# A hybrid transformer block on one core: inputs in the host's layouts, and a start without transposes of x

## The chip, the cores and the metric

The kernel runs on one core of one Trainium2 chip. The metric is the device time of one execution in microseconds (us), the median of several runs. A profile was taken of one further execution; its trace has the start and length of each instruction on the engines TensorE (PE), VectorE (DVE), ScalarE (ACT) and GpSimd (POOL), of SyncE (SP) and of the DMA queues.

## What is computed

One layer of a block over 256 tokens of 2048 features, in float32. Cut to what matters:

```
h = rms_norm(x, mix_norm)
proj = h @ w_in                               # 2048 -> 10320 columns
dn_q, dn_k, dn_v, dn_z, dn_b, dn_a, mla_q, mla_ckv, mla_kr, gate_a, gate_b = split(proj)
# branch A: conv of 4 taps + SiLU on q, k, v; l2-normed q, k; gated delta rule in chunks of 64
q_a, k_a = l2norm(cq), l2norm(ck)
o_a = gated_delta_rule(q_a, k_a, v_a, g, beta)      # holds a triangular solve in each chunk
# branch B: attention over a compressed KV latent, block-causal mask
o_b = mla_attention(qn, qr, kn, kr, v_b)
y = sigmoid(gate_a) * (o_a @ w_branch_a) + sigmoid(gate_b) * (o_b @ w_branch_b)
x = x + y @ w_out
x = x + square(relu(rms_norm(x, mlp_norm) @ w_mlp_up)) @ w_mlp_down     # 2048 -> 8192 -> 2048
x = x + sigmoid(rms_norm(x, ple_norm) @ w_ple_gate) * (p @ w_ple)
```

where `rms_norm(x, g)` is `x * rsqrt(mean(x * x) + eps) * g`.

## The kernel before

**The stream.** All weights pass through one loop, `stream(groups)`. A *group* is one product of 256 tokens with 512 columns of a weight (464 in the first group, 384 in the query groups of branch B), and a *step* is two blocks of 128 rows of its weight: a raw tile of 128 x 2 x 512 floats, 512 KB, that SP loads (`load`, five raw buffers). `cut` splits it three steps ahead: ACT casts it to the fast float format (`whi`, a group at L102, the line through which all ACT and DVE instructions are recorded), and DVE subtracts (`wlo`). The activations are held in the same way, high and low. A product takes three matmuls, high by high, high by low and low by high, so a step has 12 matmuls of up to 512 columns (L392; L385 and L388 for groups with the operands turned). There are 540 steps. Sums of a group lie in two banks of a PSUM pool of four; the other pool of four serves everything else (`bank`).

**Side work.** Between steps `weave` lets one of four lanes of generators go on: L_TURN (making the activations), L_CONV (convolutions of q, k, v and loading of parameters), L_SOLVE (the triangular solve and the delta rule) and L_MLA. A scheduler then sets each engine's order, by the program's order and by what waits for what. Up to the point where the row statistic `rx` is known, ACT and DVE keep strictly to the program's order (`act.on`, `dve.on`).

**The start.** x is loaded with tokens on the partitions in four pieces (`load_x`) between the first raw tiles. TensorE turns it, 32 transposes of 128x128 (`tp_hT`, L269). ACT scales the result by the gain `mix_norm` into the high part of `hT` and DVE makes the low part. The gains come as rows of a small tile (`gmix`) and are turned too (`tp_mix`). The sum of squares of each token comes from ACT's squares of x with a running sum (`junk_x`), and `rx` is its rsqrt by Newton steps on DVE. `rx` is applied where a group leaves PSUM. The first group's `evac_first` begins with `until(lambda: "rx" in done)`, so the program's order puts all that leads to `rx` ahead of the second group. The first group carries the columns of the decay gates; their sums over tokens, `gsum` (L713), go to TensorE as 12 small matmuls. The first group's sums are used by branch A and B; after the second group, the third is of 384 columns.

**The middle.** Each of k, q, v is convolved in two halves (`conv`). For k, TensorE turns the result to tokens (`tp_tmk`, L757), ACT squares it (`junk_k`), DVE takes the rsqrt (`l2k`, `l2kv`, `l2ky`, `rk`) and multiplies (`tmk`), and TensorE turns it back (`tp_kT`, L781), the operand of `kk` (L820). The triangular solve sends diagonal blocks through DRAM by GpSimd's queue and back (`there`, to `blk`), works them row by row on DVE (`blk`), and sends the results back (`back`, to `ro`), from which DVE masks the diagonal blocks (`d`).

**Parameters.** Gains, conv weights, a_log, dt_bias, rope gains and positions come as twelve small loads in `load_rest`, behind the rest of the constants; the gains and conv weights are turned on TensorE (`gain_columns`).

The two lines that set the order around the change are these:

```
            until(lambda: "rx" in done)           # first line of evac_first
            if k0 + 2 >= g.nk: g.evac(ps)         # in stream: a group leaves at its last step
```

Of the kernel before, what the change touches and what calls it, by code (L numbers as in the profile page):

```python
# [9 lines left out]
F32 = mybir.dt.float32  # L10
# [30 lines left out]
NPIECE = 5  # L41

# [47 lines left out]


# [17 lines left out]
def hybrid_block(ctx: ExitStack, tc: tile.TileContext, a, dbg=None):  # L109
# [3 lines left out]
    x, out = a["x"][0], a["out"][0]  # L113
    w_in = a["w_in"][0]
# [32 lines left out]

    cst = cpool.tile([P, CST.shape[1]], F32, name="cst")
    nc.sync.dma_start(cst[:, :P], a["cst"][:, :P])
    gmix = big("gmix", shape=(KD, P))  # L150
    nc.scalar.dma_start(gmix, a["mix_norm"][0].rearrange("(r p) -> r p", p=P))
# [9 lines left out]

    rows = (("mlp_norm", 16), ("ple_norm", 16), ("ckv_norm", 4),
            ("dn_out_norm", 1), ("q_nope_norm", 1), ("k_nope_norm", 1))
    nrows = sum(n for _, n in rows)
    rowt = big("rowt", shape=(P, 2, P))
    grow, crow = rowt[:nrows, 0, :], rowt[:96, 1, :]
    gcol, r0 = {}, 0
    for name, n in rows:
        gcol[name] = r0
        r0 += n  # L170
    gains = cpool.tile([P, nrows + KD], F32, name="gains")
    gcol["mix_norm"] = nrows
    convw = cpool.tile([P, 96], F32, name="convw")
    hw = cpool.tile([P, 16], F32, name="hw")
    rg = cpool.tile([P, 2, ROPE], F32, name="rg")
    posi = cpool.tile([P, NT], I32, name="posi")

    def load_rest():
        def load(dst, src):
            tc.keep_in_program_order(nc.sync.dma_start(dst, src))  # L180

        load(cst[:, P:], a["cst"][:, P:])
        yield
        for name, n in rows:
            r0 = gcol[name]
            load(grow[r0 : r0 + n, :], a[name][0].rearrange("(r p) -> r p", p=P))
            yield
        load(crow, a["conv_w"][0].rearrange("k (c p) -> (k c) p", p=P))
        yield
        load(hw[:, 0:8], a["a_log"][0].partition_broadcast(P))  # L190
        load(hw[:, 8:16], a["dt_bias"][0].partition_broadcast(P))
        yield
        load(rg[:, 0, :], a["q_rope_norm"][0].partition_broadcast(P))
        load(rg[:, 1, :], a["k_rope_norm"][0].partition_broadcast(P))
        with nc.allow_non_contiguous_dma(reason="256 positions"):
            load(posi, a["positions"][0].rearrange("(b p) -> p b", p=P))
        yield


    tp = bank("tp_mix")  # L200
    pe.transpose(tp[:, :KD], gmix, ident[:KD, :KD])
    dve.tensor_copy(gains[:, nrows:], tp[:, :KD])

    def gain_columns():
        tp = bank("tp_gain")
        pe.transpose(tp[:, :nrows], grow, ident[:nrows, :nrows])
        pe.transpose(tp[:, 64:160], crow, ident[:96, :96])
        dve.tensor_copy(gains[:, :nrows], tp[:, :nrows])
        dve.tensor_copy(convw, tp[:, 64:160])
        yield  # L210

    def gain(name, k=0):
        c = gcol[name] + k
        return gains[:, c : c + 1]
# [70 lines left out]


# [36 lines left out]
    class Group:  # L323


        def __init__(self, acts, w, c0, n, nk, evac, before=None, w2=None, turned=None):
            self.acts, self.w, self.c0, self.n, self.nk = acts, w, c0, n, nk
            self.evac, self.before, self.w2, self.turned = evac, before, w2, turned

    def stream(groups):  # L330
        steps = [(g, k) for g in groups for k in range(0, g.nk, 2)]
        raws, parts = {}, {}

# [875 lines left out]
```

## Time and profile before

| what | value |
|---|---|
| time, median of 3 runs | 1586.31 us (1586.22 to 1587.17) |
| profiled execution | 1588.33 us |
| span of its trace | 1585.2 us |
| bytes by DMA | 284.86 MB, mean 180 GB/s |
| packets under 2 KB / under 8 KB, of all | 25598 / 154686, of 154788 |
| TensorE rows | 7877 matmuls |

A row of the timeline has the start and the busy time in us, the engine, the line of the kernel, the operation, out<-in with shapes and how many stand in the row, and in brackets the idle time ahead of it and what ended that. A row of the chain has start, length, engine, tile and line. Names with a `q` behind the engine (SPq, ACTq) are its instructions that issue DMAs. The span leaves out 3.1 us of the profiled execution.

### The profile page before, as it was taken

The page shows a single profiled execution, that of the slowest core. Times are in us where ns is not written, and L with a number is a line of the kernel's source. Part 1 is how long each engine was busy: PE and PEld are TensorE (multiplying, and loading weights), DVE is VectorE, ACT ScalarE, POOL GpSimd, SP SyncE. Part 2 cuts the span into 40 slices and gives each one's busy share as a digit, 9 for nine tenths or more (in the row PEclk, how much of TensorE's full clock was granted, in tenths as well). Part 3 has the DMA queues.
Part 4 walks back from the last instruction along what each step waited for, and adds up shares of the span by engine and source line. Part 5 has one row for each costly group of instructions (what it writes and reads, how often), then busy time and mean ns, then how long its engine had stood idle before and what let it go on. Part 6 is the DMA issues. An engine that isn't in the chain of part 4 may idle for free.

```text
span 1585.2 us, 21028 instructions
## 1 busy us (share of the span) xinstructions
PE 1565.1 (99%) x7877; PEld 1323.5 (83%) x7877; DVE 975.2 (62%) x1685; ACT 778.7 (49%) x1200; POOL 10.9 (1%) x21
## 2 busy tenths in 40 slices
PE   7999999999999999999999999999999999999998
PEld 6898888788888888888888888888888888888888
DVE  4987677764775654755566665456544665455554
ACT  5766676544534454445444443344433443344543
POOL 0000000000000000000000000000000000000000
PEclk9999999999999999999999999999999999999999
DMA  8555544454454565565666655565556655555553
GB/s 269 156 189 174 152 140 126 147 160 146 149 189 149 158 185 194 178 239 186 186 186 188 188 184 199 189 194 189 193 186 188 189 184 197 193 181 183 186 205 114
DMA packets 154788, 284.86 MB, mean 180 GB/s; under 512 B 12263, under 2 KB 25598, under 8 KB 154686
## 3 DMA queue, kind: packets, MB, share of 16 engines
q1 hardware_dynamic: 153550, 281.94, 55.5%
q8 instruction: 61, 1.00, 0.3%
q10 hardware_dynamic: 752, 1.06, 0.2%
q0 software_dynamic: 384, 0.53, 0.2%
q14 instruction: 41, 0.34, 0.1%
HBM read 281.13 MB, written 2.36 MB: 179 GB/s over the span
## 4 chain that ended last, share of the span: by engine, by line
PE 92%; issue 2%; DVE 2%; ACT 2%; DMA 2%; SPq 0%; POOL 0%; DVEq 0%; ACTq 0%; POOLq 0%
PE ps L392 64%; PE ps L385 15%; PE ps L388 8%; DVE wlo L102 1%; ACT whi L102 1%; PE tx L895 1%; DMA raw<-in_w_in 0%; PE td L903 0%; DMA x<-in_x 0%; PE sc L636 0%; PE te L890 0%; PE sc L637 0%; DMA blk<-there 0%; DMA ro<-back 0%; PE vn L942 0%
## 5 line engine op out<-in xcount | busy, mean ns | idle before, releaser
L102 DVE TENSOR_TENSOR wlo<-raw,whi 128x1024 fp32r<-128x1024 f32 (+3 forms) x540 | 644.6, 1195 | 503.5 <-ACT whi L102 502.4
L102 ACT CAST whi<-raw 128x1024 fp32r<-128x1024 f32 (+3 forms) x540 | 555.0, 1029 | 730.4 <-PE ps L392 501.1
L392 PE MATMUL ps<-whi,hT 128*128 128x512 f32 (+2 forms) x1344 | 426.1, 389 | 2.2 <-ACT hT L102 1.7
L392 PE MATMUL ps<-whi,uT 128*128 128x512 f32 x1024 | 319.4, 392 | 0.0
L392 PEld LDWEIGHTS ps<-whi,hT 128*128 128x128 f32 x1344 | 252.8, 189 | 46.5 <-ACT hT L102 2.6
L385 PE MATMUL ps<-nT,whi 128*128 128x512 f32 x1024 | 280.0, 394 | 0.0
L392 PE MATMUL ps<-wlo,hT 128*128 128x512 f32 (+2 forms) x672 | 258.5, 385 | 0.0
L392 PEld LDWEIGHTS ps<-whi,uT 128*128 128x128 f32 x1024 | 192.1, 188 | 42.4
L392 PE MATMUL ps<-wlo,uT 128*128 128x512 f32 x512 | 201.0, 392 | 0.0
L385 PEld LDWEIGHTS ps<-nT,whi 128*128 128x128 f32 x1024 | 175.1, 189 | 23.6 <-DVE x L102 0.5
L388 PEld LDWEIGHTS ps<-nT,wlo 128*128 128x128 f32 x1024 | 157.2, 189 | 22.0
L388 PE MATMUL ps<-nT,wlo 128*128 128x256 f32 x1024 | 163.4, 281 | 0.0
L392 PEld LDWEIGHTS ps<-wlo,hT 128*128 128x128 f32 x672 | 127.4, 190 | 20.1 <-issue 0.2
L392 PEld LDWEIGHTS ps<-wlo,uT 128*128 128x128 f32 x512 | 96.2, 188 | 21.3
L392 PE MATMUL ps<-whi,gT 128*128 128x512 f32 (+1 forms) x320 | 82.3, 347 | 0.0
L392 PE MATMUL ps<-whi,yT 128*128 128x512 f32 x256 | 79.7, 391 | 0.0
L392 PEld LDWEIGHTS ps<-whi,gT 128*128 128x128 f32 x320 | 56.1, 189 | 7.6
L392 PEld LDWEIGHTS ps<-whi,yT 128*128 128x128 f32 x256 | 47.9, 188 | 9.7
L392 PE MATMUL ps<-wlo,gT 128*128 128x512 f32 (+1 forms) x160 | 55.5, 347 | 0.0
L392 PE MATMUL ps<-wlo,yT 128*128 128x512 f32 x128 | 50.1, 391 | 0.0
L392 PE MATMUL ps<-whi,obT 128*128 128x512 f32 x128 | 40.7, 393 | 0.0
L392 PE MATMUL ps<-whi,oaT 128*128 128x512 f32 x128 | 40.7, 394 | 0.0
(483 smaller groups left out, 1194.5 us busy)
## 6 DMA issues: line engine op xcount, KB each, us to landing
raw<-in_w_in SPq DMA_DIRECT2D x136, 512.0 KB, 3.5
raw<-in_w_mlp_up SPq DMA_DIRECT2D x128, 512.0 KB, 3.7
raw<-in_w_mlp_down SPq DMA_DIRECT2D x128, 512.0 KB, 3.5
raw<-in_w_out SPq DMA_DIRECT2D x32, 512.0 KB, 3.5
raw<-in_w_ple_gate SPq DMA_DIRECT2D x24, 512.0 KB, 3.5
raw<-in_w_in SPq DMA_DIRECT2D x24, 384.0 KB, 3.2
raw<-in_w_branch_b SPq DMA_DIRECT2D x16, 512.0 KB, 3.7
raw<-in_w_branch_a SPq DMA_DIRECT2D x16, 512.0 KB, 3.6
```

The lines of the kernel that those rows point to most:

```text
L102: i = f(*args, **kwargs)
L385: pe.matmul(ps[c], hi[:, j, cs], g.acts.both(k), start=first, stop=False)
L388: pe.matmul(ps[c][:, :T], lo[:, j, cs], g.acts.both(k)[:, :T], start=False, stop=last)
L392: pe.matmul(ps[tb], g.acts.at(k, part, tb), w[:, j, : g.n], start=(first and n_ == 0), stop=(last and n_ == 2),)
L895: pe.matmul(ps[:, h, :], off[tb][:, h * P : (h + 1) * P], cols[tb][:, h, :], start=True, stop=True)
```

## The change

The host hands over other layouts. x comes a second time, feature by feature (`xT`), with its first two blocks and the gains `mix_norm` apart in one piece (`xT0`, 270 KB, on ACT's queue). p comes turned (`pT`). All small parameters come as one piece (`par`, 144 KB), and the constants as one (873 KB), both after the x pieces. The weights come as one flat array in the order in which the steps use them: each step is one contiguous piece, 4 KB for each of 128 partitions, and the first step is loaded and split in two halves.

On the chip the transposes of x, p, gains and conv weights go. ACT scales x straight from the loaded tiles. TensorE starts with `NSPIN` = 14 matmuls of 512 columns on a tile of zeros that POOL sets first. The squares for `rx` are made by ACT on whole tiles, added by DVE (three additions of tiles and of halves in all), and summed over the partitions by two matmuls with ones (`xsum`). A group that ends before `rx` is known leaves later, at the start of a step after `rx` is known. `part` is renamed `bind`.

```diff
+    first_x = big("first_x", shape=(P, XG + KD))
+    nc.scalar.dma_start(first_x, a["xT0"])
+    def load_xT(j):
+        if x_quad[j // 2] is None:
+            x_quad[j // 2] = big(f"xT{j // 2}", shape=(P, 4, T))
+        x_pair[j] = x_quad[j // 2][:, 2 * (j % 2) : 2 * (j % 2) + 2, :]
+        nc.sync.dma_start(x_pair[j], a["xT"][:, 2 * j : 2 * j + 2, :])
     cst = cpool.tile([P, CST.shape[1]], F32, name="cst")
-    nc.sync.dma_start(cst[:, :P], a["cst"][:, :P])
-    gmix = big("gmix", shape=(KD, P))
-    nc.scalar.dma_start(gmix, a["mix_norm"][0].rearrange("(r p) -> r p", p=P))
+    spin = big("spin", shape=(P, 512))
+    nc.gpsimd.memset(spin, 0.0)
+    ones = cpool.tile([P, 2], F32, name="ones")
+    nc.gpsimd.memset(ones, 1.0)
+    idle = bank("idle")
+    for _ in range(NSPIN):
+        pe.matmul(idle, spin[:, :P].bitcast(F32R), spin.bitcast(F32R), start=True, stop=True)
...
         def load(i):
-            for w, c0, n in g.w2 or [(g.w, g.c0, g.n)]:
-                nc.sync.dma_start(t[:, :, at : at + n],
-                    w[k * P : (k + 2) * P, c0 : c0 + n].rearrange("(k p) n -> p k n", p=P))
+            src = a["weights"][offs[i] : offs[i] + 2 * P * n].rearrange("(p k n) -> p k n", p=P, k=2)
+            if i == 0:
+                for k in range(2):
+                    nc.sync.dma_start(t[:, k, :n], src[:, k, :])
+            else:
+                nc.sync.dma_start(t[:, :, :n], src)
...
         for i in range(min(RAW_BUFS, n)):
-            if i < 4:
-                x_in.append(load_x(i, nc.sync))
             load(i)
+            if i < 3:
+                load_xT(i + 1)
+        for j in range(4, 8):
+            load_xT(j)
         L_CONV.add(load_rest())
         for i in range(min(AHEAD, n)):
+            L_TURN.step()
             cut(i)
-            if i < 2:
-                weave(True)
-        ps = None
+        ps, late = None, None
         for i, (g, k0) in enumerate(steps):
+            if late and "rx" in done:
+                late()
+                late = None
...
             if k0 + 2 >= g.nk:
-                g.evac(ps)
+                if "rx" in done:
+                    g.evac(ps)
+                else:
+                    assert late is None
+                    late = bind(g.evac, ps)
...
     def normed():
-        for n in range(4):
-            yield from hT.fill(4 * n, x_in[n], [gain("mix_norm", 4 * n + k) for k in range(4)])
-        for n in range(4):
-            for tb in range(NT):
-                squares(x_in[n][:, tb, :], ss0[:, tb, n : n + 1], f"x{n}{tb}")
-            yield
-        dve.tensor_copy(rx, total_rsqrt(ss0, "rx"))
+        for j in range(8):
+            hi, lo = hT.alloc(j)
+            for k in range(2):
+                act.activation(hi[:, k, :], x_pair[j][:, k, :], AF.Copy, scale=gain("mix_norm", 2 * j + k))
+            for k in range(2):
+                dve.scalar_tensor_tensor(lo[:, k, :], x_pair[j][:, k, :], gain("mix_norm", 2 * j + k),
+                                         hi[:, k, :].bitcast(F32), ALU.mult, ALU.subtract)
+            hT.ready.update((2 * j, 2 * j + 1))
+            yield
...
+                act.activation(sq, x_quad[n], AF.Square)
...
+                dve.tensor_tensor(sums[n - 1], sums[n - 1], sq, ALU.add)
+        yield
+        tot = sums[0]
+        dve.tensor_tensor(tot, tot, sums[2], ALU.add)
+        dve.tensor_tensor(tot[:, 0:2, :], tot[:, 0:2, :], tot[:, 2:4, :], ALU.add)
+        dve.tensor_tensor(tot[:, 0, :], tot[:, 0, :], tot[:, 1, :], ALU.add)
+        yield
+        ps = bank("xsum")
+        for tb in range(NT):
+            pe.matmul(ps[:, 2 * tb : 2 * tb + 2], tot[:, 0, tb * P : (tb + 1) * P], ones, start=True, stop=True)
+        yield
+        dve.tensor_copy(rx, rsqrt(ps[:, 0 : 2 * NT : 2], NT, 1.0 / D, EPS, "rx"))
     def evac_first(ps):
-        until(lambda: "rx" in done)
```

What an engine runs is set by the scheduler, so the order of instructions shows more than the diff. A row below has the line, the operation, out<-in, the shape, and how many alike follow each other. TensorE's start before, down to the first group's first products (`ps_0` and `ps_1` are its two banks):

```order
L201 MATMUL tp_mix<-cst,gmix 128x16
L269 MATMUL tp_hT__142<-cst,x_109 128x128 x4
L269 MATMUL tp_hT__178<-cst,x_109 128x128 x4
L269 MATMUL tp_hT__208<-cst,x_114 128x128 x4
L269 MATMUL tp_hT__238<-cst,x_114 128x128 x4
L392 MATMUL ps_0_162<-whi_132,hT_141 128x464
```

And TensorE's start after the change:

```order
L210 MATMUL idle<-spin 128x512 x14
L425 MATMUL ps_0_175<-whi_145,hT_140 128x464
L425 MATMUL ps_0_175<-wlo_146,hT_140 128x464
L425 MATMUL ps_0_175<-whi_145,hT_140 128x464
L425 MATMUL ps_1_176<-whi_145,hT_140 128x464
```

The 16 first transposes and the one of the gains are gone from ahead of the first product, and the spin stands there.

DVE before, around the first use of the transfer for the first half's solve (`blk` of 64x1) and the normalising of the second half of k (`l2ku`, `rk`, `tmk`):

```order
L102 TENSOR_SCALAR l2ky<-l2kh 128x8
L102 SCALAR_TENSOR_TENSOR l2ku<-l2ky 128x8
L102 TENSOR_TENSOR blk_3142<-blk_3142 64x1
L102 TENSOR_TENSOR l2ku<-l2ku,l2kv 128x8
...
L102 COPY rk_3219<-l2ky 128x8
L102 TENSOR_TENSOR blk_3142<-blk_3142 64x5x5
L102 TENSOR_TENSOR tmk_3117<-tmk_3117,rk_3219 128x512 x2
```

The same place after the change; between the last two rows printed stand three more wlo and six rows of the next convolution (`cvq`):

```order
L142 COPY rk_3134<-l2ky 128x8
L142 TENSOR_TENSOR qk_3139<-kk_3140,dt_3089 128x128
L142 TENSOR_TENSOR tmk_3027<-tmk_3027,rk_3134 128x512 x2
L142 TENSOR_TENSOR wlo_3183<-raw_3099,whi_3182 128x1024
...
L142 TENSOR_REDUCE ri_3206<-db_3207 128x64
L142 TENSOR_REDUCE ri_3206<-db_3210 128x64
...
L142 TENSOR_TENSOR blk_3215<-blk_3215 64x1
```

Before, `blk` of 64x1 stood ahead of most of the k chain and of `tmk`; now it stands behind both.

DVE before, at the end of the second solve, where `d` waits for the results (`ro`):

```order
L102 TENSOR_REDUCE blk_4431<-blk_4431 64x15
L102 TENSOR_TENSOR wlo_4575<-raw_4530,whi_4574 128x1024
L102 TENSOR_TENSOR gb_3843<-ps_0_4506,gb_3843 128x512
L102 TENSOR_TENSOR gb_3843<-ps_1_4507,gb_3843 128x512
L102 TENSOR_TENSOR wlo_4601<-raw_4554,whi_4600 128x1024
L102 TENSOR_TENSOR d_16_4680<-ro_4620,cst 128x128 x3
L102 TENSOR_TENSOR wlo_4625<-raw_4578,whi_4624 128x1024
```

And after the change:

```order
L142 TENSOR_REDUCE blk_4458<-blk_4458 64x15
L142 TENSOR_TENSOR wlo_4651<-raw_4604,whi_4650 128x1024
L142 TENSOR_TENSOR wlo_4669<-raw_4630,whi_4668 128x1024
L142 TENSOR_TENSOR d_16_4706<-ro_4646,cst 128x128 x4
L142 TENSOR_TENSOR n_16_4707<-at_4303,cst 128x512
L142 TENSOR_TENSOR wlo_4687<-raw_4654,whi_4686 128x1024
```

The two operations on the gates (`gb`) between the solve's end and the wait have moved behind it, and two wlo stand ahead of it as before.

More of the change, by code (lines that the diff above doesn't have):

```diff
@@ L41 @@
 NPIECE = 5
+NSPIN = 14
 def _round12(v):
@@ L89, with _parameters, _by_feature, _packed_weights @@
 CST, AT = _constants()
+ROWS = (("mlp_norm", 16), ("ple_norm", 16), ("ckv_norm", 4),
+        ("dn_out_norm", 1), ("q_nope_norm", 1), ("k_nope_norm", 1))
+GCOL, NROWS = {}, 0
+for _name, _n in ROWS:
+    GCOL[_name] = NROWS
+    NROWS += _n
+P_CONV = NROWS
+P_HW = P_CONV + 96
+P_RG = P_HW + 16
+P_POS = P_RG + 2 * ROPE
+NPAR = P_POS + NT
+XG = 2 * T
+def _parameters(v):
+    by_p = lambda a: np.ascontiguousarray(np.asarray(a, np.float32).reshape(-1, P).T)
+    every = lambda a: np.broadcast_to(np.asarray(a, np.float32).reshape(1, -1), (P, a.size))
+    cols = [by_p(v[name][0]) for name, _ in ROWS]
+    cols.append(by_p(v["conv_w"][0]))
+    cols += [every(v["a_log"][0]), every(v["dt_bias"][0]), every(v["q_rope_norm"][0]), every(v["k_rope_norm"][0])]
+    pos = np.ascontiguousarray(np.asarray(v["positions"][0], np.int32).reshape(NT, P).T)
+    cols.append(pos.view(np.float32))
+    return np.ascontiguousarray(np.concatenate(cols, axis=1))
+def _by_feature(a, nk):
+    return np.ascontiguousarray(np.asarray(a, np.float32).T.reshape(nk, P, T).transpose(1, 0, 2))
+def _packed_weights(steps, v):
+    out = []
+    for srcs, k in steps:
+        out.append(np.concatenate([v[name][0][r0 + k * P : r0 + (k + 2) * P, c0 : c0 + n].reshape(2, P, n)
+                                   for name, r0, c0, n in srcs], axis=2).transpose(1, 0, 2).reshape(-1))
+    return np.ascontiguousarray(np.concatenate(out), np.float32)
 class InOrder:
@@ L160, in hybrid_block @@
     ident = C("ident")
[L162 to L173, printed above, removed]
@@ L174, in hybrid_block @@
-    hw = cpool.tile([P, 16], F32, name="hw")
-    rg = cpool.tile([P, 2, ROPE], F32, name="rg")
-    posi = cpool.tile([P, NT], I32, name="posi")
+    convw = par[:, P_CONV:P_HW]
+    hw = par[:, P_HW:P_RG]
+    rg = par[:, P_RG:P_POS].rearrange("p (a b) -> p a b", a=2)
+    posi = par[:, P_POS:].bitcast(I32)
     def load_rest():
-        def load(dst, src):
-            tc.keep_in_program_order(nc.sync.dma_start(dst, src))
-        load(cst[:, P:], a["cst"][:, P:])
+        tc.keep_in_program_order(nc.sync.dma_start(par, a["par"]))
@@ L195, in load_rest @@
[L195 to L209, printed above, removed]
+        tc.keep_in_program_order(nc.sync.dma_start(cst, a["cst"]))
@@ L210, in gain_columns @@
         yield
     def gain(name, k=0):
-        c = gcol[name] + k
-        return gains[:, c : c + 1]
+        if name == "mix_norm":
+            return first_x[:, XG + k : XG + k + 1]
+        c = GCOL[name] + k
+        return par[:, c : c + 1]
     def rsqrt(src, n, mul, add, name, post=None):
@@ L284, in fill @@
                 yield
+    bind = lambda f, *args: (lambda *more: f(*args, *more))
     class Lane:
@@ L527, in work @@
         def work():
-            yield from gain_columns()
             yield from rotary_tables()
@@ L1093, in hybrid_block @@
-    wu, wd, wg, wp = a["w_mlp_up"][0], a["w_mlp_down"][0], a["w_ple_gate"][0], a["w_ple"][0]
+        groups.append(Group(yT, wo, 512 * n, 512, KD, bind(evac_wo, n), before=reload_x if n == 0 else None))
+    wu, wd, wg, wp = "w_mlp_up", "w_mlp_down", "w_ple_gate", "w_ple"
     state = {}
@@ L1137, in load_p @@
     def load_p():
-        t = big("pt", shape=(P, NT, T))
-        nc.sync.dma_start(t, a["p"][0][0].rearrange("(b p) d -> p b d", p=P))
+        t = big("pt", shape=(P, 2, T))
+        nc.sync.dma_start(t, a["pT"])
         yield
         yield
-        yield from pT.fill(0, t)
+        split(*pT.alloc(0), t)
+        pT.ready.update((0, 1))
+        yield
     def evac_pw(n, ps):
```

133 lines of the change are left out of this document (71 added, 62 removed).

## The prediction

> **What bounds the kernel now.** I read the page's busy shares first, then its forty slices and its chain of work, and only then the trace.
>
> ```profile
> PE 1565.1 (99%) x7877; PEld 1323.5 (83%) x7877; DVE 975.2 (62%) x1685; ACT 778.7 (49%) x1200; POOL 10.9 (1%) x21
> PE   7999999999999999999999999999999999999998
> PE 92%; issue 2%; DVE 2%; ACT 2%; DMA 2%; SPq 0%; POOL 0%; DVEq 0%; ACTq 0%; POOLq 0%
> 577.62 61.69 PE ps L392 x272
> raw<-in_w_in SPq DMA_DIRECT2D x136, 512.0 KB, 3.5
> ```
>
> TensorE is busy for 99% of the span, carries 92% of the chain, and only the first and last of the slices are below 9. The fourth line is one link of the chain: 272 matmuls of 128x512 in 61.69 us, so 0.2268 us each at full clock. None of the big matmuls goes away here, so the change can win only where TensorE is idle, at a low clock, or doing transposes. The table of windows (length, then busy time and count of PE, PEld, DVE, ACT and POOL, granted clock, DMA share, GB/s) shows the start, one settled stage, and the one place in the middle that lost something.
>
> ```profile
> 0.00:5.00 5.00, 0.26 (x1) 0.18 (x1) 0.23 (x2) 1.48 (x2) 1.91 (x8) 1.00 0.51 142
> 5.00:10.00 5.00, 3.24 (x14) 2.84 (x15) 1.13 (x1) 0.97 (x1) 0.00 (x0) 1.00 1.03 349
> 10.00:15.00 5.00, 3.94 (x12) 3.14 (x11) 2.87 (x4) 2.67 (x4) 0.00 (x0) 1.00 1.07 374
> 960.00:1000.00 40.00, 40.00 (x178) 33.11 (x178) 20.37 (x19) 15.77 (x15) 0.00 (x0) 1.00 0.55 191
> 280.00:320.00 40.00, 36.96 (x174) 30.32 (x173) 31.09 (x90) 21.06 (x41) 2.11 (x3) 0.91 0.45 139
> ```
>
> In the settled stage nothing is to be had: TensorE is full and the DMA engines are at 0.55. The first 15 us are bound by transfers (share over 1, 349 to 374 GB/s), and 280 to 320 holds 3.04 us of idle TensorE and a granted clock of 0.91. So the sum has two main terms.
>
> **Term 1, the start: up to the third group.** Before, these rows lead to the first 384-column matmuls:
>
> ```profile
> 0.75 0.42 ACTq L151 DMA_DIRECT2D gmix<-in_mix_norm  x1
> 1.00 1.45 POOL L589 MEMSET qrT<- 64x512 f32 x3
> 2.86 0.18 PEld L201 LDWEIGHTS tp_mix<-cst,gmix 16*128 16x128 f32 x1 [2.86 <-DMA gmix<-in_mix_norm]
> 6.00 1.11 PE L269 MATMUL tp_hT__142<-cst,x 128*128 128x128 f32 x4 [2.86 <-DMA x<-in_x]
> 7.42 0.97 ACT L102 CAST whi<-raw 128x928 fp32r<-128x928 f32 x1 [4.74 <-DMA raw<-in_w_in]
> 11.75 0.76 PE L392 MATMUL ps<-whi,hT 128*128 128x464 f32 x1 [1.06 <-ACT hT L102]
> 12.69 0.59 PE L392 MATMUL ps<-whi,hT 128*128 128x464 f32 x1
> 13.08 0.59 PE L392 MATMUL ps<-wlo,hT 128*128 128x464 f32 x1
> 15.47 0.38 PE L392 MATMUL ps<-wlo,hT 128*128 128x464 f32 x1
> 18.86 0.37 PE L392 MATMUL ps<-wlo,hT 128*128 128x464 f32 x1
> 25.13 0.37 PE L392 MATMUL ps<-wlo,hT 128*128 128x464 f32 x1
> 28.07 0.60 PE L269 MATMUL tp_hT__296<-cst,x 128*128 128x128 f32 x4
> 28.50 0.60 PE L269 MATMUL tp_hT__325<-cst,x 128*128 128x128 f32 x4
> 49.50 0.17 DVE L102 COPY rx<-rxy 128x2 f32<-128x2 f32 x1
> 59.66 1.48 PE L713 MATMUL gsum<-gate,cst 128*128 128x8 f32 x12 [0.96 <-issue]
> 62.18 0.34 PE L392 MATMUL ps<-wlo,hT 128*128 128x384 f32 x1
> ```
>
> A 464-column matmul starts every 0.39 us at 12.69 and 13.08 and lasts 0.38 from 15.47 on against 0.59 before: the clock comes up at about 15 us. Between 18.86 and 25.13 stand 30 matmuls, so 0.209 us each. A 512-column one at the low clock then takes 0.39 x 512 / 464 = 0.43.
>
> After the change TensorE first runs 14 matmuls on zeros. They wait for POOL's memset of a 128x512 tile, which is now the first; the three there take 1.45, so 0.48 each and the spin starts at about 1.5. All cold it lasts 14 x 0.43 = 6.0 and ends at 7.5; if the clock rises midway it ends nearer 6.2. The first real operands are 270 KB of x with the gains and 237 KB of weights (half of the first step). gmix, a small transfer, was there at 2.86; 507 KB at 374 GB/s add 1.36, so 4.2 at best. At worst they queue with the transfers behind them: 6.0, where the first x of before arrived. Add 1.4 for ACT's scaled copy, its cast of the half (0.97 / 2) and the hand-over: 5.6 to 7.4. I take the first real matmul at **7.0**, just as the spin ends.
>
> From there: group 1, 96 x 0.209 = 20.06; group 2, 96 x 0.2268 = 21.77; the gate sums, now behind the third group's first matmuls without a wait, still as 1.34 of work; two small matmuls with ones for the squares, 0.5. That is 43.7, plus 0.3 for the first steps' wlo and 0.7 for a wait of the small matmuls on the new squares, which the rows of before do not show. Their nearest rows bound that wait:
>
> ```profile
> 30.37 0.85 ACT L102 ACTIVATE hT<-tp_hT__325,gains 128x256 fp32r<-128x256 f32 x2
> 31.65 0.87 DVE L102 SCALAR_TENSOR_TENSOR hT<-tp_hT__325,gains,hT 128x256 fp32r<-128x256 f32 x2
> 33.24 1.22 DVE L102 TENSOR_TENSOR wlo<-raw,whi 128x1024 fp32r<-128x1024 f32 x1 [0.71 <-ACT whi L102]
> 36.57 0.63 ACT L102 ACTIVATE junk_x<-x 128x512 f32<-128x512 f32 x1
> ```
>
> Four squares of whole tiles at up to 2 x 0.63 and three additions at 1.2, 0.6 and 0.35 (by the width of the 1.22 row) are 7 us of work on two engines, spread over six steps of 2.5 to 2.7 us; each step also takes 0.85 and a cast on ACT, 0.87 and 1.22 on DVE. It fits (wait 0) unless it bunches up (2.5 us, one step); 0.7 is nearer the first. Sum: 7.0 + 43.7 + 1.0 = **51.7**, against 62.0 before (the 62.18 row follows its group's first matmul by 0.17). Gain **10.3**, between 8.5 (the wait at 2.5, operands at 7.4) and 11.8 (operands at 5.6, no wait).
>
> That sum already has the 32 transposes of x in it: 0.43 us from 28.07 to 28.50 for four, so 0.109 warm, and cold 0.28. The deferred eviction costs nothing there: group 2 uses the other bank pool, group 3 needs the first pool only at 51.7, and the row statistic (rx, at 49.50 before) should be there by 41, three steps into group 2 and then its rsqrt. If it came after 50, TensorE would wait.
>
> Here a rule of the Trainium skill speaks against so short a spin. The Trainium skill, TensorE: Matmul & The Clock Gate, Part 1 (The HAM clock gate), says the clock rises after one busy window of about 3.4 us whose phase is free-running. A spin of 6.0 us is sure to hold a whole such window only from 6.8 on; by that rule the clock may rise as late as 8.2, and the sum would lose 0.6 at most. The trace does not contradict it: about 4 us of matmuls, 11 to 15, brought the clock up.
>
> **Term 2, the middle: the stall at 282 us.**
>
> ```profile
> 266.06 0.39 PE L820 MATMUL kk<-cvq,cvk 128*128 128x128 f32 x2
> 273.20 1.09 PE L757 MATMUL tp_tmk<-cst,cvk 128*128 128x128 f32 x8
> 278.81 0.17 DVE L102 TENSOR_SCALAR l2kv<-l2k 128x8 f32<-128x8 f32 x1 [0.24 <-ACT junk_k L102]
> 282.04 0.15 DVE L102 TENSOR_TENSOR blk<-blk 64x1 f32<-64x1 f32 x1 [2.44 <-DMA blk<-there]
> 284.93 1.29 DVE L102 TENSOR_TENSOR tmk<-tmk,rk 128x512 f32<-128x512 f32 x2
> 285.77 0.66 PE L781 MATMUL tp_kT<-cst,tmk 128*128 128x128 f32 x2 [3.04 <-DVE tmk L102]
> 288.36 0.63 PE L392 MATMUL ps<-wlo,hT 128*128 128x512 f32 x1
> 289.64 0.63 PE L392 MATMUL ps<-wlo,hT 128*128 128x512 f32 x1
> ```
>
> DVE waits 2.44 us for a transfer of the triangular solve, and the normalising of k (l2k to tmk) stands behind that wait in its order. TensorE reaches the transposes of k, is idle for 3.04 us, and then runs at half clock: 3 matmuls in 1.28 us from 288.36, 0.427 each. A mean clock of 0.91 over the 40 us of the window means 40 x 0.09 / 0.5 = 7 us at one half; with some 1 of them before TensorE went on, 6 us of its work ran at half rate and 2.9 were lost. Together 5.9.
>
> In the new order on DVE the k chain and tmk stand ahead of the first operation that needs the transfer, with six rows of the next convolution and four wlo between. The round trip is then hidden behind work. TensorE comes to the transposes of k after what stands between in the new order: 27 matmuls (6.1), 12 transposes (1.3) and 8 small products (kk, at most 0.2 each, 1.6): 9.0, or 9.6 with the hand-overs between them, behind tp_tmk's start. DVE's tmk was 284.93 - 273.20 = 11.7 behind it with the wait of 2.44; without it 9.3, plus the first half, 0.65: 9.6 to 10.2. Left over is a wait of 0.4 (0 to 1.5), which I take as too short to bring the clock down. Gain **5.5**, 4.4 to 5.9.
>
> **Smaller terms.**
>
> ```profile
> 450.11 0.70 DVE L102 TENSOR_TENSOR d<-ro,cst 128x128 f32<-128x128 f32 x3 [3.98 <-DMA ro<-back]
> 451.99 0.50 PE L392 MATMUL ps<-wlo,obT 128*128 128x512 f32 x1 [1.35 <-DVE wlo L102]
> ```
>
> At 450 DVE waits 3.98 us for the solve's results, and the wlo behind it comes 1.35 us late. In the new order two wlo stand between the solve's last row and that wait, so DVE is a step further ahead when it stops: gain **1.4**, 0 to 1.7. The four transposes of p go: 4 x 0.109 = **0.4**. Packing the weights changes rows of 2 KB to rows of 4 KB; a step's 512 KB landed 3.5 us after issue with five steps of 2.7 us in flight, so a faster transfer gains **nothing**, and a slower one costs nothing until a step takes over 2.7 us. The parameters and constants, whole and later, land beside group 1's weights; their first users are past 52 us.
>
> Against this stands what a wholly new order brings. DVE is the fullest engine beside TensorE from 62 to 320 us (31.09 of 40 in the 280 window), and the side work shifts by some 10 us against the stream there. I allow **-2** for waits that are not there now, between 0 and -8; the lower end is one more stall with the half clock (5.9) and some short ones.
>
> **Sum.** 10.3 + 5.5 + 1.4 + 0.4 - 2 = 15.6. The profiled run took 1588.33 (span 1585.2 and 3.1 around it), so it becomes 1572.7. The median of the runs, 1586.31, is 2.0 lower; by that measure **1570.7**.
>
> **Rivals.**
> - *A new stall takes the place of the old one.* Another product or transpose that waits over 3 us for DVE between 62 and 450 brings the half clock with it and costs 5.9 again: 1576.6, and two of them 1582.5. For it: DVE's load there, and that one such stall arose before. Against it: the waits now stand behind more queued work.
> - *The spin does nothing.* Zeros might not count as work, or the span of waiting between spin and operands may be too long. For it: the transposes of x filled 3.24 of the 5 us from 5 on and did not lift the clock. Then group 1 begins at half rate for 4 us as before (11 to 15), 2 us lost: 1572.7.
> - *Slower: the packed loads.* If loads of 4 KB rows ran below 512 KB in 2.72 us, 193 GB/s while in flight (now 191 at a share of 0.55, so about 345 at full share), TensorE would wait in every step. That is the point from which it decides. At half the present rate, 172 GB/s, a step takes 3.04 instead of 2.72, and the 1500 us behind the start grow by 12%: about 1750. Against it: nothing in the table of windows shows that longer rows are slower.
> - *The change misses its aim at the start*: the operands come with the whole queue, at 10 instead of 7. Costs 3: 1573.7.
>
> **How the numbers follow.** My forecast, with new waits of up to 4 us and no half clock, 1566.5 to 1574.5: 0.47. The rival of the spin: 0.07, and that of late operands: 0.08, both inside the same stretch, which so holds 0.62. A new stall: 0.25, 1574.5 to 1581. Several stalls, or one and a failed start, 1579 and up to no difference: 0.05, of which 0.03 above 1583.1. Packed loads, or a like price in every step: 0.04. Below 1566.5, if all waits vanish: 0.04. The range 1566 to 1579 leaves out about 0.2. A measurement of this kernel can tell 0.2%, 3.2 us, from no change; so faster means below 1583.1: 0.93, the same 0.03, slower 0.04.
>
> **What would show it.** Right if the first group's matmul of 464 columns comes at about 7 with 0.37 each soon after, the third group starts near 52, the small matmuls on the squares wait under 1 us, and the windows around the second convolution of k have a granted clock of 1.00. Wrong if there is an idle TensorE of over 3 us anywhere between 62 and 450, if the settled windows have less than 40.00 busy, or if group 3 waits for the first group's banks.

## The result and the profile after

| | before | after |
|---|---|---|
| time, median | 1586.26 us (4 runs, 1585.18 to 1587.17) | 1571.24 us (4 runs, 1570.80 to 1572.15) |
| ratio to before | 1 | 0.9905 (95%: 0.9890 to 0.9921) |
| span of the profiled execution | 1585.2 us | 1569.0 us |

The change takes 15.0 us from the median and 16.2 us from the span. 1570.7 was predicted, with a range of 1566 to 1579. The total is right; two of the reasons behind it are not, as the experiments show.

The page of after, in the rows that were read before:

```profile
PE 1559.6 (99%) x7856; PEld 1319.2 (84%) x7856; DVE 976.6 (62%) x1687; ACT 775.7 (49%) x1190; POOL 11.4 (1%) x23
PE   9999999999999999999999999999999999999998
PE 93%; DVE 3%; ACT 2%; DMA 1%; issue 1%; DVEq 0%; ACTq 0%
raw<-in_weights SPq DMA_DIRECT2D x492, 512.0 KB, 3.3
```

The first of the forty slices rose from 7 to 9. TensorE's busy time fell by only 5.5 us, so most of the gain is idle time that went (20.1 us of the span before, 9.4 after). The windows of after (length; busy and count of PE, PEld, DVE, ACT, POOL; granted clock; DMA share; GB/s):

```profile
5.00:10.00 5.00, 5.00 (x20) 4.11 (x18) 3.06 (x7) 3.62 (x8) 0.00 (x0) 1.00 0.99 326
10.00:15.00 5.00, 4.32 (x21) 3.65 (x20) 4.25 (x7) 4.04 (x7) 0.00 (x0) 1.00 1.05 401
960.00:1000.00 40.00, 40.00 (x178) 33.15 (x177) 20.43 (x19) 15.64 (x15) 0.00 (x0) 1.00 0.55 191
260.00:300.00 40.00, 39.84 (x205) 32.95 (x203) 34.55 (x93) 27.92 (x60) 2.19 (x3) 1.00 0.52 171
```

TensorE works from 5 us on, the settled stage is as it was (40.00 busy, 0.55 of the DMA engines, 191 GB/s), and around the second convolution of k the clock is 1.00, with 0.16 us idle. TensorE's waits, first three of the ten rows of before (the others are mostly waits of the start, as in the prediction's rows) and then those of after (engine, what waits, what for: us in all, times, longest):

```profile
PE tp_kT L781 <- DVE tmk L102: 3.5, 2, 3.0
PE ps L392 <- DVE wlo L102: 1.3, 1, 1.3
PE gsum L713 <- issue: 1.0, 1, 1.0
```

```profile
PE idle L210 <- POOL spin L205: 1.4, 1, 1.4
PE xsum L485 <- DVE xsq L142: 1.2, 1, 1.2
PE ps L425 <- DVE wlo L142: 0.7, 1, 0.7
PE gsum L772 <- DVE gate L142: 0.6, 1, 0.6
PE tp_kT L840 <- DVE tmk L142: 0.5, 2, 0.3
PE tp_tmv L816 <- ACT cvv L142: 0.5, 1, 0.5
```

The list of after is complete for waits of over 0.15 us: under 5 us, of which 1.4 are the time until the spin can start. The timeline of after places them (start, busy, engine, line, operation, in brackets the idle time and its end):

```profile
1.35 6.20 PE L210 MATMUL idle<-spin 128*128 128x512 f32 x14 [1.35 <-POOL spin L205]
7.39 0.37 PE L425 MATMUL ps<-whi,hT 128*128 128x464 f32 x1
10.97 0.47 PE L425 MATMUL ps<-wlo,hT 128*128 128x464 f32 x1 [0.68 <-DVE wlo L142]
37.95 0.61 PE L485 MATMUL xsum<-ones,xsq 128*128 128x2 f32 x4 [1.18 <-DVE xsq L142]
52.30 0.34 PE L425 MATMUL ps<-wlo,hT 128*128 128x384 f32 x1
54.46 1.51 PE L772 MATMUL gsum<-gate,cst 128*128 128x8 f32 x12 [0.58 <-DVE gate L142]
```

The first real product starts at 7.39, at full clock (0.37 a matmul), and the third group begins at 52.1 instead of 62.0.

### The profile page after: what moved, and what is told of

It is laid out like the page before. It is cut to its first block, busy times and chain, and to the rows that moved or that the text cites. A ratio compares the mean times of both kernels' runs of the same rounds, so it can differ in the third digit from the quotient of the medians.

```text
span 1569.0 us, 20945 instructions
## 1 busy us (share of the span) xinstructions
PE 1559.6 (99%) x7856; PEld 1319.2 (84%) x7856; DVE 976.6 (62%) x1687; ACT 775.7 (49%) x1190; POOL 11.4 (1%) x23
## 4 chain that ended last, share of the span: by engine, by line
PE 93%; DVE 3%; ACT 2%; DMA 1%; issue 1%; DVEq 0%; ACTq 0%
PE ps L425 65%; PE ps L418 15%; PE ps L421 8%; DMA raw<-in_weights 1%; DVE wlo L142 1%; PE tx L954 1%; ACT whi L142 1%; PE td L962 0%; DVE blk L142 0%; PE te L949 0%; DVE cvv L142 0%; ACT junk_k L142 0%; DMA first_x<-in_xT 0%; PE sc L696 0%; PE sc L695 0%
```

## The experiments

Each ran beside the kernel before on the same chip; the ratio of that pair is what counts, since the kernel before moved between 1586.0 and 1587.1 from chip to chip. The 95% intervals are within 0.0017 of the ratio, some 2.7 us; smaller differences are read from the traces, by how much earlier or later the same cast or product of a weight starts in two kernels, which shows where one falls behind another. A span is that of one execution. Where the clock falls can differ between executions of one kernel (last section): of a_early's four, one has a span of 1576.6 and a mean clock of 0.998, the others 1579.3 to 1580.5 and 0.995.

| run | what it is | median, us | ratio to before | span, us |
|---|---|---|---|---|
| (after) | the change | 1571.24 | 0.9905 | 1569.0 |
| b_order | before, order on DVE put right at 282 | 1581.99 | 0.9966 | 1578.6 |
| b_late | before, deferred eviction alone | 1580.59 | 0.9958 | 1577.3 |
| b_spin | before, spin alone | 1586.49 | 0.9992 | 1583.4 |
| b_packed | before, packed weights alone | 1585.46 | 0.9998 | 1583.9 |
| a_early | after, without the deferral | 1581.45 | 0.9962 | 1580.5 |
| a_early_order | a_early, order on DVE put right | 1577.29 | 0.9949 | 1575.1 |
| a_nospin | after, without the spin | 1571.42 | 0.9902 | 1570.0 |
| a_unpacked | after, weights in their own layout | 1575.12 | 0.9924 | 1573.5 |
| a_xsum1 | after, xsum a step later, one turn more | 1572.75 | 0.9907 | 1571.2 |
| a_xsum1_nospin | the same without the spin | 1573.63 | 0.9914 | 1571.9 |
| a_xsum_only | after, xsum a step later, turns as before | 1570.70 | 0.9908 | 1568.6 |
| a_xsum_only_unp | the same with unpacked weights | 1574.03 | 0.9928 | 1571.7 |

### The stall at 282: is it the order on DVE?

b_order, the kernel before with this edit (and `dve.on` off again behind each piece):

```diff
         dve.memset(sol ... 1.0)
         yield
         yield
         yield
+        for _ in range(2 if half == 0 else 0):
+            yield
         for i in range(1, BASE):
+            dve.on = half == 0 and i == 1
...
         if kind in "qk":
+            dve.on = kind == "k" and half == 1
             r = rsqrt(ss, 8, ...)
```

> The kernel before, with one thing moved: on DVE the normalising of the second half of k stands ahead of the first use of the solve's transfer. If the stall at 282 comes from that order (theory), TensorE's wait of 3.0 us and the half clock behind it (2.9) both go: 1586.3 - 5.9 = 1580.4, and the windows around 282 have a clock of 1.00. Rival 1: the stall went because the start or the loads changed; then the time stays at 1586 within 1 and TensorE still waits about 3 us there. Rival 2: the solve, now later, makes a wait of its own further on: a gain under 3.

The ratio is 0.9966 (0.9953 to 0.9979), 5.4 us by the ratio and 6.6 by the spans. Of these 6.6, 0.4 stand at the start already, 4.7 arise at the stall and 1.5 at 450, where b_order no longer has before's wait of 1.35. In the timeline of b_order TensorE's wait for k is 0.58 instead of 3.04, and the window around it has a clock of 1.00:

```profile
282.74 0.41 PE L783 MATMUL tp_kT<-cst,tmk 128*128 128x128 f32 x2 [0.58 <-DVE tmk L102]
```

```profile
270.00:290.00 20.00, 19.42 (x96) 15.25 (x96) 15.60 (x31) 14.85 (x33) 2.19 (x3) 1.00 0.58 169
```

So the stall was the order, and it goes with nothing else changed than this order and the first half's solve, which comes two turns later. What the change does to that order is the next question.

### Which part of the change moves that order?

b_late is the kernel before with the deferral alone, and a_early is the changed kernel without it:

```diff
# b_late, against before            # a_early is the same turned round, against after
+            if late and "rx" in done:
+                late()
+                late = None
...
-                g.evac(ps)
+                if "rx" in done:
+                    g.evac(ps)
+                else:
+                    assert late is None
+                    late = lambda f=g.evac, p=ps: f(p)
     def evac_first(ps):
-        until(lambda: "rx" in done)
```

> The kernel before with the deferred eviction alone (old layouts, transposes of x, no spin). Theory: the deferral by itself moves the side work of the lanes behind the stream, so that DVE's order has the normalising of k ahead of the solve's transfer; the 5.9 us of the stall at 282 go, and the gate sums' wait of 1.0 as well: 1579 to 1580.5, clock 1.00 around 282. Rival: it is the earlier start and the new layouts that move the order, and the deferral alone leaves the stall: 1585 to 1586.

> The changed kernel, but the first group leaves PSUM in the program's order before the second, as before the change. Theory: at the start nothing changes by more than 1 us (the third group starts at 52 to 53), but the side work starts sooner against the stream, and DVE's order has the first use of the solve's transfer ahead of the normalising of k again: 5.9 come back there with a clock below 1, 1577.1. Rival: the deferral pays at the start, TensorE waits 3 to 6 us in the second group for the squares (third group at 55 to 58) and the middle stays at full clock: 1574 to 1577 as well, but told apart by where.

b_late: 0.9958 (0.9943 to 0.9973), 6.7 us by the ratio and 7.9 by the spans, with waits of only 0.5 for k. Its order is close to that of after, so the two also show what the rest of the change is worth: after is 7.3 ahead of b_late when the third group is under way, at 62 to 70, and 8.4 at the end. No run takes that rest apart, into the transposes of x, the loads in one piece and the order of the loads. a_early: 0.9962 (0.9947 to 0.9976), that is 9 us above the changed kernel by the ratios and 11.5 by the spans. The timeline of a_early has the old stall again, now at 283, and a second one at the start:

```profile
37.60 1.01 PE L481 MATMUL xsum<-ones,xsq 128*128 128x2 f32 x4 [3.60 <-DVE xsq L142]
279.62 0.15 DVE L142 TENSOR_TENSOR blk<-blk 64x1 f32<-64x1 f32 x1 [2.49 <-DMA blk<-there]
283.35 0.66 PE L837 MATMUL tp_kT<-cst,tmk 128*128 128x128 f32 x2 [3.10 <-DVE tmk L142]
```

The deferral, not the layouts, moves the order: alone it removes the stall, and without it the stall is back. And it does something at the start too, against the theory: with the early eviction, program order puts the matmuls on the squares (xsum) earlier in the second group, TensorE waits 3.60 us for them, and the clock falls for two stretches. In the windows of a_early:

```profile
36.60:43.40 6.80, 5.80 (x16) 4.73 (x17) 5.03 (x22) 0.27 (x1) 0.00 (x0) 0.50 0.44 140
280.00:300.00 20.00, 16.90 (x72) 13.78 (x71) 17.44 (x53) 9.36 (x14) 0.00 (x0) 0.83 0.30 108
```

Theory and rival were each half right. a_early_order puts DVE's order right in a_early, by the edit of b_order, to take the two halves apart:

> The changed kernel with the early eviction again, but with DVE's order around the solve's transfer put right by hand. Theory: of the 10 to 11 us that the early eviction cost, the stall of k with its half clock (6) goes and the start's part remains (a wait of 3.6 at 38 instead of 1.2, with the half clock behind it): 1575.5 to 1576.5. Rival: the stall's cost comes back at another place: 1580 or more.

0.9949 (0.9934 to 0.9964): 5.4 us of span less than a_early and 6.1 more than after. The stall at 283 is gone, the wait of 3.6 at 38 remains. Not all of the 5.4 are the order in the middle: 1.1 are there by 45 us already, since its clock fell for one stretch (39.3 to 42.7) where a_early's fell for two, 4.7 arise at the stall, as in b_order, and 0.5 are lost further on. So of the 11.5 by which a_early is longer than after, 4.7 are the order in the middle, and the rest is the start and branch B. Its third group begins at 57.1, with the gate sums done; after begins it at 52.1 and spends 1.9 on the gate sums and their wait behind that, so some 3 of its 6.1 are the start. Most of the other 3 are waits of branch B that after does not have:

```profile
PE tp_kn L674 <- DVE kn L142: 1.5, 3, 0.7
PE tp_qr L641 <- DVE rot L142: 0.6, 1, 0.6
```

### What is the spin worth?

a_nospin sets `NSPIN = 0` in the changed kernel; b_spin puts the 14 matmuls of zeros into the kernel before:

```diff
+    spin = big("spin", shape=(P, 512))
+    nc.gpsimd.memset(spin, 0.0)
+    idle = bank("idle")
+    for _ in range(14):
+        pe.matmul(idle, spin[:, :P].bitcast(F32R), spin.bitcast(F32R), start=True, stop=True)
```

> The changed kernel without the 14 matmuls of zeros. Theory: the first product starts at about 6.2 instead of 7.4 and runs at half clock; its 12 matmuls last 4.7 us, to 10.9, when the second step's wlo arrives (10.97) whatever the clock is. What is lost is only what runs at half clock after 11: 0 to 1.5 us, 1571.2 to 1572.7. Rival (the prediction's price for a spin that does nothing): 2 us and more, 1573.2 to 1575. Rival 2: the spin is worth nothing at all and its matmuls even cost: 1570 or less.

> The kernel before with the 14 matmuls of zeros ahead of the transposes of x. Theory: the clock is up at about 7 and the transposes and products from 5.6 to 15 run at full rate, but the products then wait for transfers and hT: a gain of 0 to 1.5, 1585 to 1586.5. Rival 1 (the prediction's price of a cold first group): 2 us less, 1584.3. Rival 2: transposes do not hold the clock; it falls back between 7 and 15, and the time is unchanged: the clock's record tells this from the theory.

a_nospin: 0.9902 (0.9887 to 0.9917), not to be told from after. In its timeline the first product starts at 5.82, cold, and the clock rises at about 10; the matmuls on the squares start at 37.93, as in after at 37.95:

```profile
5.82 0.75 PE L425 MATMUL ps<-whi,hT 128*128 128x464 f32 x1 [5.82 <-ACT whi L142]
9.37 0.84 PE L425 MATMUL ps<-whi,hT 128*128 128x464 f32 x2
10.05 0.37 PE L425 MATMUL ps<-wlo,hT 128*128 128x464 f32 x1
37.93 0.58 PE L485 MATMUL xsum<-ones,xsq 128*128 128x2 f32 x4 [1.50 <-DVE xsq L142]
```

What TensorE does before 38 decides nothing: without the spin it waits 1.50 there, with it 1.18, and from then on the two kernels run within 0.05 us of each other until 450. (The 1.0 between their spans arises at 450 to 458, where the results of the second solve come at 451.6 instead of 450.6; more on this below.) The spin lifts the clock, as forecast, and is worth nothing here.

b_spin: 0.9992 (0.9983 to 1.0002), no difference. Its windows show why:

```profile
5.00:8.50 3.50, 2.91 (x17) 2.07 (x15) 0.17 (x1) 0.94 (x1) 0.00 (x0) 1.00 1.00 350
8.50:11.90 3.40, 1.38 (x9) 1.16 (x10) 1.83 (x2) 1.73 (x4) 0.00 (x0) 1.00 1.05 358
11.90:15.30 3.40, 3.40 (x10) 2.92 (x9) 2.33 (x4) 0.97 (x2) 0.00 (x0) 0.50 1.08 374
```

The clock is up from 5 on, but in 8.5 to 11.9 TensorE has only transposes and waits (1.38 busy), and then it falls to one half just as the products begin. That is the outcome that rival 2 forecast. The Trainium skill, TensorE: Matmul & The Clock Gate, Part 4 (PE-mode transpose), says that transposes do not count as busy in the way products do; this run does not contradict it, but with 2 us of idle time in the same window it can't separate the two.

### The wait for the squares

Three kernels move the two matmuls on the squares a step later. a_xsum1 puts one more `yield` ahead of them; a_xsum1_nospin drops the spin as well; a_xsum_only takes a `yield` away behind them, so that the side work has as many turns as in after:

```diff
+        yield                       # all three
         ps = bank("xsum")
         for tb in range(NT):
             pe.matmul(ps[:, 2 * tb : 2 * tb + 2], tot[:, 0, ...], ones, start=True, stop=True)
-        yield                       # a_xsum_only
         dve.tensor_copy(rx, rsqrt(...))
```

> The changed kernel with the two small matmuls on the squares one step later in the second group. Theory: they alone make TensorE wait at the start (1.18 us at 38), since the chain of casts, squares and additions on ACT and DVE ends at 38 whatever TensorE does; one step later (2.7 us) it is done: the wait goes, 1.2 less, 1570.0, and the third group starts at 51. Rival: the chain that follows (rx, the eviction, the gate sums) is late in its place and takes it back: 1571.2.

> Both: the small matmuls one step later and no spin. Theory: without the spin TensorE reached the small matmuls 0.3 us sooner (wait of 1.50 instead of 1.18), so with the wait gone the spin costs 0.3 net: 1569.7, 0.3 below the run with the spin. Rival: the spin's worth was hidden by that wait and shows now: 1 us above the run with the spin.

> The small matmuls on the squares one step later, but with as many turns of the side work as in the changed kernel, so that TensorE's order is the same from the eviction on. Theory: the 1.18 us of the wait at 38 go and nothing else moves: 1570.0, no half clock up to 1560. Rival: the clock falls behind the gate sums at 55 to 58, as in the run with one turn more, and takes 1.7 back: 1571.5 to 1572.

a_xsum1, 0.9907 (0.9891 to 0.9924): the wait is gone, but the clock falls behind the gate sums, and the shifted order costs further on: 0.5 ahead of after at 65, it is 2.2 behind at the end, and most of that arises between 430 and 570. The rival's outcome came, but through the half clock and the order, and not through a longer wait at the gate sums (0.58, as in after). a_xsum1_nospin, 0.9914, whose clock falls at the same place (57.6 to 61.1), is 0.2 to 0.4 behind a_xsum1 from the first group on, and 0.7 at the end; the rival's sign is right, its size (1) is not, and the theory's 0.3 the other way is wrong. In the windows of a_xsum1:

```profile
55.10:58.60 3.50, 2.92 (x21) 2.85 (x21) 2.52 (x30) 3.42 (x8) 0.00 (x0) 0.99 0.70 221
58.60:62.00 3.40, 3.40 (x12) 3.40 (x12) 3.40 (x30) 2.94 (x4) 0.00 (x0) 0.51 0.02 6
```

a_xsum_only, 0.9908 (0.9893 to 0.9924): the trace bears the theory out up to 450, where it is 1.4 ahead of after. It then gives 1.2 of that back. The timelines of a_xsum_only and of after at the second solve:

```profile
450.32 0.90 DVE L142 TENSOR_TENSOR d<-ro,cst 128x128 f32<-128x128 f32 x4 [5.19 <-DMA ro<-back]
451.88 1.06 PE L954 MATMUL tx<-ro,n 128*128 128x16 f32 x8 [0.27 <-DVE n L142]
456.76 1.06 PE L954 MATMUL tx<-ro,n 128*128 128x16 f32 x8 [0.27 <-DVE n L142]
```

```profile
450.57 0.90 DVE L142 TENSOR_TENSOR d<-ro,cst 128x128 f32<-128x128 f32 x4 [5.27 <-DMA ro<-back]
```

The solve's results come at 450.3 and 450.6, wherever TensorE stands: it comes 1.4 earlier and waits for the solve. In these two, in a_nospin and in before, `d` starts 8.0 to 8.1 behind the solve's last row on DVE (`blk` of 64x15, at 442.3, 442.5, 443.6 and 442.1). What sets the time of that last row was not tested. None of these kernels is faster than the change.

### What is the packing worth?

a_unpacked and a_xsum_only_unp load the weights from their own arrays, with rows of 2 KB; b_packed packs them in the kernel before, with the same order on TensorE and DVE:

```diff
-            src = a["weights"][offs[i] : offs[i] + 2 * P * n].rearrange("(p k n) -> p k n", p=P, k=2)
...
-                nc.sync.dma_start(t[:, :, :n], src)
+            at = 0
+            for name, r0, c0, m in g.srcs:
+                src = a[name][r0 + k0 * P : r0 + (k0 + 2) * P, c0 : c0 + m].rearrange("(k p) n -> p k n", p=P)
...
+                    nc.sync.dma_start(t[:, :, at : at + m], src)
+                at += m
```

> The changed kernel with the weights in their own layout: each step's load has rows of 2 KB (two of 400 and 64 columns in the first group) as before. Theory: no difference beyond 0.5 us, 1571.2, since a step's weights land long before they are used. Rival 1: packing pays where the start is bound by transfers; the second step's weights land later than 8.8 us and the first group ends 1 to 3 us later: 1572 to 1574. Rival 2: rows of 4 KB move slower and only their cover hides it: the settled windows then show a lower DMA share without packing.

> The same with the weights in their own layout. Theory: of the 3.9 to 4.5 us that the layout cost, 2.7 were the longer wait at 39 (1.05) and the half clock that this wait brought (1.7); with the small matmuls a step later they go, and 1 to 1.8 above the run with packed weights remain: 1571 to 1572. Rival: 2 KB rows cost in every step; then all of the 3.9 to 4.5 remain: 1574 to 1574.5.

> The kernel before with the packed weights alone; the order of instructions on TensorE and DVE is the same. Theory: at the start, where transfers bind, they go some 7% faster and x arrives 0.3 to 1 us earlier; nothing else waits for weights: 1585.3 to 1586. Rival: rows of 4 KB are worth the 3.9 that their absence cost in the changed kernel: 1582.4.

a_unpacked, 0.9924 (0.9908 to 0.9941), is 3.0 us above after by the ratios and 4.5 by the spans. The intervals of the ratios overlap, but on the same chip a_nospin, which is level with after, took 1571.1 to 1571.8 and a_unpacked 1574.5 to 1575.5, so it is not nothing. In its windows and its timeline:

```profile
15.00:20.00 5.00, 5.00 (x26) 4.49 (x25) 3.31 (x7) 3.01 (x6) 0.00 (x0) 1.00 1.09 381
39.50:42.90 3.40, 3.40 (x10) 2.73 (x10) 3.12 (x11) 0.00 (x0) 0.00 (x0) 0.50 0.46 134
```

```profile
39.04 0.63 PE L489 MATMUL xsum<-ones,xsq 128*128 128x2 f32 x4 [2.23 <-DVE xsq L142]
```

In 15 to 20 the transfers run at 381 GB/s instead of after's 402:

```profile
15.00:20.00 5.00, 5.00 (x26) 4.50 (x25) 3.55 (x7) 3.25 (x7) 0.00 (x0) 1.00 1.04 402
```

The chain of loads, casts and squares ends 1.1 us later, TensorE waits 2.23 instead of 1.18, and that longer wait takes the clock down for 3.4 us, 1.7 lost. That makes the 2.7 by which the third group is late. The rest arises in two steps at 270 and 450 (1.4) and in small amounts later (0.5). Why the chain ends later is open between two things that the edit changes together: the length of the rows, and the number of loads. In the first group each step is now two loads, of 400 and 64 columns, and SP is done with issuing the last four pieces of x at 12.0 instead of 9.7. In the settled stage (960 to 1000) the DMA share is 0.60 against 0.55, not lower, so rival 2 is out.

a_xsum_only_unp, 0.9928 (0.9911 to 0.9945), missed the theory: it stays 3.1 behind a_xsum_only by the spans, not 1 to 1.8. The wait is gone from 39 but reappears at the gate sums, 1.6 us, and the half clock with it:

```profile
PE gsum L776 <- DVE gate L142: 1.6, 1, 1.6
```

```profile
56.60:60.10 3.50, 3.50 (x13) 3.50 (x12) 3.36 (x22) 3.43 (x7) 0.00 (x0) 0.51 0.00 0
```

So the later chain was paid at the next instruction that waits for its end. b_packed, 0.9998 (0.9988 to 1.0008): no difference. Its loads too run at 402 GB/s in 15 to 20, but its first group ends no earlier: in its timeline the products still last 0.59, the time at the low clock, at 16.49, where before had 0.38 from 15.47 on:

```profile
16.49 0.59 PE L410 MATMUL ps<-whi,hT 128*128 128x464 f32 x1
17.61 0.37 PE L410 MATMUL ps<-wlo,hT 128*128 128x464 f32 x1
```

The clock rises 2 us later there, which costs TensorE about 1 us and may hide a gain of the loads: at 45 to 50 the two kernels are level. Between 61.4 and 64.8 b_packed then has a stretch of half clock that before has not, and falls 1.3 behind. At the stall its clock falls for one stretch and before's for two, and it is level again, within 0.1. And it lacks the wait of 1.35 at 450. What the packing would be worth in the kernel before with the same clock stays open.

## Why the prediction was right, and where it was not

**What bounds the kernel**: right. The settled windows didn't move, and the gain came from the start and the one stall.

**Term 1, the start, 10.3.** The third group begins 9.9 earlier, but the forecast had the 1.34 of the gate sums inside its 51.7, and after has them behind 52.1: like for like the gain is 62.0 - 52.1 - 1.36 = 8.5, at the lower end of its bounds. (From the terms that the forecast names, the bounds are 8.1 and 12.4, not 8.5 and 11.8; and a cold transpose took 0.23 by the starts, 6.00 to 6.91 for four, not 0.28. Neither moves the sum.) Mis-sized by 0.4 to 0.5 each were the first product (7.4 against 7.0) and the waits (wlo 0.7 against 0.3, xsum 1.18 against 0.7), so that the sign "wait under 1 us" was missed; the other 0.5 lies within the two groups. The wait of the squares was taken from too short a sum: it has "three additions at 1.2, 0.6 and 0.35", 2.2 us, but the kernel makes three of whole tiles (1.22 each) and then one of a half and one of a quarter (0.69 and 0.42), 4.8 us on DVE, the last of them just ahead of the wait. The view by tile has (shortest, middle and longest in ns, first and last start in us):

```profile
L142 DVE TENSOR_TENSOR xsq<-xsq,xsq x3: 1215/1215/1216, 29.4 to 35.5; 128x1024 f32<-128x1024 f32 x3
```

Two steps behind this term failed. "The deferred eviction costs nothing there" left out that it gains: a_early_order puts its worth at the start at some 3 us, through the wait for the squares (3.60 instead of 1.18) and the clock that falls behind it, and at as much again in waits of branch B. That is so in the changed kernel alone: in the kernel before, the deferral by itself (b_late) gained 0.5 by the third group. And the price of a spin that does nothing, 2 us, was wrong: a_nospin loses none of it up to 450, because the chain that ends in the squares, not TensorE, sets when the second group goes on. The forecast counted TensorE's matmuls from 7.0 and added the wait of the squares as a remainder; it is the other way round, and TensorE's share before 38 us has slack of 1.2. By the prediction's estimate from the rule of the Trainium skill, TensorE: Matmul & The Clock Gate, Part 1 (The HAM clock gate), half rate was possible until 8.2; the first product at 7.39 took 0.37, full rate, and the clock mattered nowhere there.

**Term 2, the stall at 282, 5.5**: right in mechanism, and close in size: 4.7 in b_order against before and in a_early_order against a_early, within the stated 4.4 to 5.9. The 2.9 for the half clock in it is that of the profiled execution, and not of each one (last section). b_order and b_late each remove the stall alone, and a_early brings it back. Its wait went from 3.04 to 0.16, where 0.4 was forecast. That the stall went because of the deferral, through the order of the side work, the forecast read from the order of instructions without naming the edit that caused it.

**Smaller terms.** The 1.35 at 450 is gone, as forecast (1.4), but that the two wlo ahead of the wait are the cause is not shown: a_early still has DVE's old order there, one wlo, the two `gb` and one wlo ahead of `d`, and yet TensorE does not wait, since the solve's results come at 444.5 and DVE waits 2.74 for them instead of 3.98:

```profile
444.52 0.70 DVE L142 TENSOR_TENSOR d<-ro,cst 128x128 f32<-128x128 f32 x3 [2.74 <-DMA ro<-back]
```

What took the wait away in after stays open. The allowance of -2 for new waits was too large: new are 0.58 at the gate sums and 0.5 at tp_tmv, and two old waits of 0.5 and 0.4 went. It made good for the 1.8 that the start fell short, which is luck. That packing gains nothing is wrong by 3 to 4.5 in the changed kernel (a_unpacked), while nothing showed in the kernel before (b_packed): it looked at the settled stage, where a step has five loads in flight, and not at the start, where the DMA share of after is 1.04 to 1.05 from 10 to 25 us.

**Rivals.** No new stall with a half clock came in the change itself. It did in six of its variants (a_early, a_early_order, a_unpacked, a_xsum1, a_xsum1_nospin and a_xsum_only_unp), and only in a_early is it the old stall of k. The packed loads are no slower: 0.55 and 191 GB/s in the settled stage, as before.

## What to carry to other kernels

Where an engine is busy for 99% and an edit ahead of it changes nothing, look for the one instruction that waits for another chain's end: what that engine gains before it is given back there. Ask of an edit that moves work by a few steps which queue orders change hundreds of microseconds later; here that was worth 4.7 us, more than half of what the start was. And a layout that is idle comfort in the settled stage can be on the path in the first 25 us, where the transfers are the bound.

## What the hardware showed unexpectedly

The clock falls in whole stretches of 3.4 us (a_unpacked: 39.5 to 42.9; a_early: two of them), and a short wait can be enough: 2.23 us in a_unpacked cost 3.4 us at one half, while waits of 1.18 (after) and 1.35 (before, at 450) cost none. In a_xsum1 a wait of only 0.58 was enough, with 12 matmuls of 8 columns behind it that the profile counts as 1.5 us busy; in after the same 0.58 and the same 12 matmuls, at 54.5, left the clock up. In every trace the clock's rises and falls lie whole multiples of 3.413 us apart (in before 79 of them, from its rise at 15.09 to its fall at 284.74), and where this grid lies differs from run to run. That decides over 1.7 us, which is more than most of the edits here are worth. b_packed and before do the same work from 58.0 to 61.4, busy for 2.42 and 2.44, with the same gate sums at 59.7 behind waits of 0.98 and 0.96. Their grids differ, and only the first of them then runs at one half:

```profile
61.40:64.80 3.40, 3.40 (x12) 3.11 (x11) 3.40 (x24) 3.23 (x5) 0.00 (x0) 0.50 0.24 66
```

```profile
61.40:64.80 3.40, 3.40 (x20) 3.27 (x19) 3.40 (x24) 3.24 (x5) 0.00 (x0) 1.00 0.29 76
```

Cut along this grid, the 14 traces have 23 stretches of 3.413 us behind which the clock falls, and each holds at most 1.48 us of TensorE's products, if transposes and products of up to 16 columns are left out. The 6380 stretches behind which it stays up hold at least 1.47. That is a count from these traces and not a tested rule. The stall at 282 shows the part of the grid too: the windows of before and of b_spin have a mean clock of 0.83 and 0.91 over 20 us, that is two stretches (6.8 us) and one (3.4 us) at one half, behind much the same wait (3.0 and 2.5):

```profile
280.00:300.00 20.00, 16.96 (x72) 13.71 (x71) 15.41 (x51) 8.32 (x12) 0.00 (x0) 0.83 0.43 129
```

```profile
280.00:300.00 20.00, 17.47 (x79) 14.00 (x78) 16.92 (x55) 9.38 (x14) 0.00 (x0) 0.91 0.44 136
```

So what the stall costs beyond its wait differs between executions of the same kernel. Of the 34 executions of the kernel before that ran beside the experiments, the five with a mean clock of 1.000 have spans of 1582.1 to 1583.4, the eleven with 0.997 of 1585.3 to 1587.6.
